# Moving the start of the float32r operands in SBUF from 32 bytes past a multiple of 64 to a multiple of 64

## The chip, the cores and the metric

One NeuronCore of one Trainium2 chip runs the whole program in a single launch. The metric is the device time of one execution in microseconds (us). Its engines are TensorE (PE in the profile; its weight loads stand apart as PEld), VectorE (DVE), ScalarE (ACT), GpSimd (POOL) and SyncE (SP), which issues most DMAs. SBUF is the on-chip memory with 128 partitions; "an address" below is a byte address within a partition, and it is the same in all 128.

## The reference

Two transformer-like blocks run over 1024 tokens of 1024 features, all in float32. The first is a mixer of three branches (gated linear attention, an mLSTM memory, an S5 state space), merged by gates, and then a SwiGLU feed-forward net. The second has a latent-attention layer and a recurrent layer, each with an attention over 256 memory vectors.

```python
def first_block(x, c, ...):
    h = rms_norm(x, pre1_w[l]) * (1.0 + sc1) + sh1
    y = hybrid_mixer(h, w_in[l], ...)                  # products with 1024 x 6.7k weights, three branches
    x = x + (1.0 + gt1) * rms_norm(y, post1_w[l])
    h = rms_norm(x, pre2_w[l]) * (1.0 + sc2) + sh2
    gate, up = jnp.split(h @ ffn_w_in, 2, axis=-1)
    x = x + (1.0 + gt2) * rms_norm((silu(gate) * up) @ ffn_w_out, post2_w[l])

def second_block(x, mem, ...):                         # two layers
    z = h @ w_in;  tok = causal_attention(...) or rg_lru_branch(...)
    y = concat([tok, memory_attention(...)]) * silu(gate)
    h = layer_norm(ALPHA * h + y @ w_out, ln_g, ln_b)
```

## The kernel before

Nearly all the arithmetic is matrix products in a split form. Each float32 operand is kept as two tiles of type float32r, a high part (the rounded value) and a low part (what the rounding left): the activations are `ah` and `al`, a slot of weights is `wh` and `wl`, and other pairs are `gh`/`gl`, the two `yb`, and the parts in `tx`. One product is three TensorE matmuls, high by high, high by low and low by high, which `mm3` (by way of `mm`, whose matmul is L120) writes one after the other. So a stationary tile of 128 columns is loaded for every matmul. `ident` marks transposes (`tr`, L127), which are float32 matmuls of another form.

The moving operand of a float32r matmul is 512 columns wide (2048 bytes of a partition) in most products: `gemm_ws` for everything that is stored with features on partitions, and the FFN's output product `ffn_out`. It is 256 columns wide in three places: the output projections `w_out_pass` and the values `in_v`, where the moving operand is a weight slot; and the sums of quarters `tx` in `ffn_in`, where the 256 columns are two runs of 128 that lie apart. A few matmuls are plain float32: the profile's shapes write both types as f32, and names tell them apart. `xc,wg` and `acc,ones` are float32, as is everything of the S5, GLA and mLSTM cores.

Weights come from DRAM through `load_w`: the slot `wr` by DMA, ScalarE rounds it to `wh`, VectorE subtracts to give `wl`. `self.e()` gives a work tile of 128 x 1028 float32, of which 1024 columns are used, from a ring of four slots.

SBUF is filled from both ends. On the left lie the constants (pool `const`), then `act` with `ah` and `al`, then the pools that a stage opens. On the right lie the pools of a section: `wraw`, `whl`, then `ev`, which holds the work tiles. Every tile takes a multiple of 32 bytes. The address of a tile is therefore the sum of the tiles below it; the constants before `act` add up to a number that is 32 past a multiple of 64, and so do the pools at the right end. The tiles behind them are multiples of 64 bytes, but for the ring of work tiles: 1028 x 4 = 4112 bytes are rounded to 4128, which is 64 x 64 + 32. All slices that TensorE reads begin at multiples of 512 bytes from their tile's start. So all float32r operands, moving and stationary, begin 32 bytes past a multiple of 64, and the four slots of the ring begin at 0 and 32 past it in turn.

The order of the work on TensorE is written by the generators of the kernel and by the order in which they are stepped. Neither they nor the DMA queue look at an address.

Of the kernel before, what the change touches and what calls it, by code (L numbers as in the profile page):

```python
# [36 lines left out]
class Once:  # L37
    """Makes each of its items when it is first asked for."""
# [13 lines left out]
class Kernel:  # L52
# [8 lines left out]
    # Work is written as generators. The main one yields after each piece of work for TensorE; a  # L61
    # side one yields how many microseconds of other TensorE work its next piece should wait for.
# [87 lines left out]
    def silu2(self, out, x):  # L150
        """2 silu(x), from the tanh that shares its table with exp."""
        self.act(out, x, AF.Tanh, scale=0.5)
        self.stt(out, out, 1.0, x, ALU.add, ALU.mult)
# [9 lines left out]
    def section(self, es, raw, hl, e, width=1024):  # L163
        """Weight slots and float32 work tiles of a section, at the right end of SBUF."""
        self.ww = width
        self.wraw = self.pool("wraw", bufs=raw, es=es, side="right")
        self.whl = self.pool("whl", bufs=hl, es=es, side="right")
        self.ev = self.pool("ev", bufs=e, es=es, side="right")

    def e(self, dt=F32):  # L170
        return self.ev.tile([128, 1028], dt, tag="e", name="e")

    def load_w(self, src, n=1024):
        """One slot of weights: raw float32 from DRAM, split into two float32r parts."""
# [8 lines left out]
    def plan_w(self, *groups):  # L183
        """The weight slots the main generator will ask for, in order, in groups used together."""
# [13 lines left out]
    def gemm_ws(self, ps, w, x, nk, woff=0, halves=(0, 1)):  # L198
        """ps[128 features, 1024 tokens] from a stationary weight slot."""
# [17 lines left out]
    def gemm_pair(self, x, nk, first, rest):  # L217
        """Two column tiles, first halves first; waits for the tasks that form x's token halves."""
# [14 lines left out]
    def psc(self, ring=None):  # L233
        """One bank of PSUM, of four in turn; or of a ring of three (0), or the fourth (1)."""
# [5 lines left out]
    def rstd(self, pool, ss, n, eps, w=1):  # L240
        """(ss / n + eps) ** -0.5 on a narrow tile."""
# [7 lines left out]
    def to_act(self, src, t):  # L249
        """Token tile [128 tokens, 1024] -> act[:, :, tokens], split."""  # L250
# [15 lines left out]
    def setup(self):  # L266
        nc, A = self.nc, self.A
        self.const = self.pool("const")
        self.drp = self.pool("dr", space=DRAM)
        self.actp = self.pool("act")  # L270
# [36 lines left out]
        self.d_gq = dr("d_gq", [4, 128, 1024])   # q, q, k, k  # L307
        self.d_gc = dr("d_gc", [2, 128, 1024])   # cumulative log decay * 16
# [12 lines left out]
    def ada_vec(self, i, p, accp, wp):  # L321
        """Steps that form row vector i >= 2 of the adaLN table, broadcast over the partitions.

        A shift is mod, a scale or gate (1 + mod) * the norm's weight."""
# [29 lines left out]
    def start(self, es):  # L354
        """The first two column tiles of the input products, with h = rms(x) scale + shift into act.

        adaLN's first scale and shift come in by pieces of 256 features, and the products follow
        feature by feature."""
# [36 lines left out]
        def ada(ws):  # L395
            """Shift and scale of a block of features, before the sum over partitions."""
# [71 lines left out]
    def mem_load(self, es):  # L468
        """The memory, transposed and split."""
        p = self.pool("mkv", es=es)  # L470
        return self.mem_split([p.tile([128, 1024], F32R, name="mem%d" % i) for i in range(4)])

    def mem_split(self, t):
        """The memory's features by blocks of 128, high and low parts; t: two tiles of each part."""
# [6 lines left out]
    def mem_kv(self, l, x, tail=None):  # L481
        """Keys and values of the memory for layer l of the second block."""
# [47 lines left out]
    def in_v(self, b, qs=(0, 1)):  # L530
        """Values of branch b in token layout."""
# [18 lines left out]
    def log_sigmoid(self, a, x):  # L550
        """x <- min(x, 0) - log(1 + exp(-|x|)); a: scratch."""
# [5 lines left out]
    def local_sums(self, out, x, p):  # L557
        """Running sums over the tokens of each chunk of 128."""
# [5 lines left out]
    def in_misc(self, p1):  # L564
        """Gate inputs of both branches; GLA's log decays and their sums within chunks."""
# [38 lines left out]
    def conv(self, o, ps, w, b):  # L604
        """Causal convolution over four tokens, from PSUM."""
# [13 lines left out]
    def in_gate(self, b, func):  # L619
        """Gate of branch b, on its finished output."""  # L620
# [15 lines left out]
    def s5_pre(self, p, pt):  # L636
        """Small per-state values, [128 = (re, im) x 64 states, 32 groups]."""
# [25 lines left out]
        self.s5t = t("t", [128, 32])       # angle in turns  # L663
# [41 lines left out]
        # decay over a block of 8 steps, its angle, and powers 0..8 and 7..0  # L705
# [19 lines left out]
    def cossin(self, co, si, x, tmp):  # L725
        """cos and sin of 2 pi x; x is overwritten by its fraction in [-1/2, 1/2]."""
# [7 lines left out]
    def s5_core(self, hb, pm, pu, pt, su, turn):  # L734
        """Groups 4 hb .. 4 hb + 3."""
# [50 lines left out]
        # blocks of 8 steps  # L786
# [36 lines left out]
    def load_sy(self, b):  # L823
        """S5 output tile b as [channel, (step in block, block)]."""
# [6 lines left out]
    def s5_glu(self, p):  # L831
        """y * sigmoid(y @ w + b)."""
# [27 lines left out]
    def branch(self, b, p, ready=None, merged=None, first=False):  # L860
        """merged += 2 sigmoid(gate) * (y @ proj); ready: the task that forms y."""
# [38 lines left out]
    def gla_pair(self, pr, p1, p2, mD, ready):  # L900
        """Two heads of gated linear attention, chunks of 128 tokens, four chunks at a time.

        Within a chunk the decay between two tokens is split at the middle of the smallest aligned
        block that holds both, so that both exponents are <= 0: one product per block size."""
# [7 lines left out]
        for u in range(2):  # L912
# [55 lines left out]
            for li, m in enumerate(sizes):  # L968
# [3 lines left out]
                else:  # L972
                    # keys to the chunk's end, queries from its start
# [63 lines left out]
    def ml_rows(self, p):  # L1037
        """Per-token gate rows, [4 heads, 1024]."""
# [24 lines left out]
    def ml_core(self, p1, p2):  # L1063
# [6 lines left out]
        # per-token columns  # L1070
# [18 lines left out]
        for pr in range(2):  # L1089
            nc.gpsimd.memset(Sz, 0.0)  # L1090
            for u in range(2):
# [8 lines left out]
                # decays: exp(b_i - m_i + i_j - b_j), zero above the diagonal  # L1100
# [76 lines left out]
    def w_out_pass(self, store, evac, final, pre=None, tail=None):  # L1177
        """y[tokens, 1024] = act^T @ w by column quarters; the tasks of final are returned.

        The last two quarters go side by side over the tokens: the tiles are finished evenly."""  # L1180
# [37 lines left out]
    def block1_end(self, es, low, G, tx, tail, done):  # L1218
        """x1 = x + (1 + gt1) rms(y) w; h2 into act and tx. low, G: float32 tiles."""
# [42 lines left out]
    def to_tx(self, src, t, rb, tx):  # L1262
        """Token tile 4 + t -> the second halves of act and the sums of quarters with token tile t."""
# [25 lines left out]
    # The hidden features come by the Strassen-Winograd scheme: seven products of quarters in place  # L1289
    # of eight. Quarters of the weights: gate and up column tile by half of the contraction; of the  # L1290
    # activations: half of the contraction by half of the tokens.
    def ff_raw(self, i, fs):
        """Weights of a pair and their sums: g = A11, A12; u = A21 -> S3, A22; s = S1, S2."""
# [30 lines left out]
    def ffn_in(self, tx, fs, a, fin):  # L1324
        """a: the first pair, its first weights loaded."""
# [28 lines left out]
        def add(out, ps, x, a, b, h=0, g=0):  # L1354
            """out <- ps + x at columns a:b of halves h, g."""
# [86 lines left out]
    def ffn_out(self, es, slot):  # L1442
# [35 lines left out]
        def out(parts):  # L1478
            """Products of one group of hidden features, or of the last two."""
# [997 lines left out]
```

## Time and profile before

| | us |
|---|---|
| median of 3 runs | 2843.36 |
| lowest, highest | 2841.15, 2856.39 |
| span of the profiled execution | 2851.6 |
| TensorE busy in it | 2711.0 (95%) |
| weight loads | 2230.4 (78%) |
| VectorE busy | 1716.1 (60%) |
| ScalarE busy | 930.2 (33%) |
| GpSimd busy | 856.5 (30%) |

The profiled execution is its own run: its span, 2851.6 us, is 8.2 us over the median. The profile gives a start and a duration for every instruction. Matmuls are pipelined, so a matmul's duration is longer than the time from its start to the start of the next. What a stream of matmuls costs is that spacing, and it is read from starts in the timeline, or from the count of matmuls in a stretch without idle time.

### The profile page before, as it was taken

The page shows a single profiled execution, that of the slowest core. Times are in us where ns is not written, and L with a number is a line of the kernel's source. Part 1 is how long each engine was busy: PE and PEld are TensorE (multiplying, and loading weights), DVE is VectorE, ACT ScalarE, POOL GpSimd, SP SyncE. Part 2 cuts the span into 40 slices and gives each one's busy share as a digit, 9 for nine tenths or more (in the row PEclk, how much of TensorE's full clock was granted, in tenths as well). Part 3 has the DMA queues.
Part 4 walks back from the last instruction along what each step waited for, and adds up shares of the span by engine and source line. Part 5 has one row for each costly group of instructions (what it writes and reads, how often), then busy time and mean ns, then how long its engine had stood idle before and what let it go on. Part 6 is the DMA issues. An engine that isn't in the chain of part 4 may idle for free. (4 is left out here: it accounts for less than half of the span.)

```text
span 2851.6 us, 40682 instructions
## 1 busy us (share of the span) xinstructions
PE 2711.0 (95%) x16156; PEld 2230.4 (78%) x16156; DVE 1716.1 (60%) x2462; ACT 930.2 (33%) x1427; POOL 856.5 (30%) x767
## 2 busy tenths in 40 slices
PE   6989899999999999799999999999989998999998
PEld 5778688778878889698988888787766665976688
DVE  7886974553453244944544456653577776667586
ACT  6453544311111133422222321232333334146330
POOL 4694661000000002844444200131213547112332
PEclk8999999899999999899999999999999999999999
DMA  8323224444564242222222422242220113322231
GB/s 243 108 73 113 92 81 134 134 134 168 185 214 164 94 146 91 89 89 88 68 89 86 151 89 89 96 164 76 92 85 29 34 42 107 139 82 64 70 107 64
DMA packets 133901, 304.10 MB, mean 107 GB/s; under 512 B 18024, under 2 KB 61880, under 8 KB 133584
## 3 DMA queue, kind: packets, MB, share of 16 engines
q1 hardware_dynamic: 133712, 301.51, 31.5%
q8 instruction: 127, 2.08, 0.3%
q14 instruction: 62, 0.51, 0.1%
HBM read 226.17 MB, written 73.94 MB: 105 GB/s over the span
## 5 line engine op out<-in xcount | busy, mean ns | idle before, releaser
L120 PE MATMUL psg<-ah,wh 128*128 128x512 f32 x1392 | 563.5, 406 | 21.6 <-ACT wh L1311 9.3
L120 PE MATMUL psg<-ah,wl 128*128 128x512 f32 x1392 | 558.0, 401 | 3.5 <-DVE wl L136 3.5
L120 PE MATMUL psg<-al,wh 128*128 128x512 f32 x1392 | 557.8, 401 | 2.1 <-DVE al L136 2.0
L136 DVE TENSOR_TENSOR wl<-wr,wh 128x1024 fp32r<-128x1024 f32 (+3 forms) x212 | 272.1, 1285 | 379.3 <-ACT wh L179 262.8
L179 ACT CAST wh<-wr 128x1024 fp32r<-128x1024 f32 (+3 forms) x161 | 162.3, 1010 | 798.7 <-PE psg L120 379.5
L120 PEld LDWEIGHTS psg<-ah,wh 128*128 128x128 f32 x1392 | 265.8, 191 | 92.7 <-issue 12.3
L120 PEld LDWEIGHTS psg<-al,wh 128*128 128x128 f32 x1392 | 266.6, 191 | 66.1 <-issue 5.5
L120 PEld LDWEIGHTS psg<-ah,wl 128*128 128x128 f32 x1392 | 266.5, 191 | 64.5 <-DVE wl L136 3.7
L120 PE MATMUL psc<-wh,ah 128*128 128x256 f32 x1024 | 290.5, 284 | 7.8 <-DVE ystore L136 4.3
L120 PE MATMUL psc<-wl,ah 128*128 128x256 f32 x1024 | 287.2, 281 | 0.0
L120 PE MATMUL psc<-wh,al 128*128 128x256 f32 x1024 | 286.7, 281 | 0.0
L142 POOL TENSOR_SCALAR rsv<-ss 128x1 f32<-128x1 f32 x32 | 12.8, 400 | 757.2 <-DVE ss L1238 514.0
L120 PEld LDWEIGHTS psc<-wh,ah 128*128 128x128 f32 x1024 | 196.7, 192 | 13.0 <-DVE ystore L136 5.0
L120 PEld LDWEIGHTS psc<-wl,ah 128*128 128x128 f32 x1024 | 195.8, 191 | 0.3
L120 PE MATMUL psc<-tx,wh 128*128 128x256 f32 x1088 | 195.5, 280 | 0.0
L120 PEld LDWEIGHTS psc<-wh,al 128*128 128x128 f32 x1024 | 195.4, 191 | 0.1
L136 POOL TENSOR_TENSOR e<-e 128x1024 f32<-128x1024 f32 (+3 forms) x65 | 110.0, 1696 | 238.5 <-issue 112.0
L120 PEld LDWEIGHTS psc<-tx,wh 128*128 128x128 f32 x1088 | 170.0, 189 | 3.3
L136 POOL TENSOR_TENSOR acc<-acc,e 128x512 f32<-128x512 f32 (+2 forms) x60 | 116.2, 1936 | 158.3 <-PE psc L120 155.9
L120 PE MATMUL psc<-tx,wl 128*128 128x256 f32 x544 | 152.8, 281 | 0.0
L136 DVE TENSOR_TENSOR e<-psc,e 128x512 f32<-128x512 f32 (+1 forms) x138 | 89.9, 666 | 103.4 <-PE psc L120 103.2
L120 PE MATMUL psc<-wh,gh 128*128 128x512 f32 x352 | 139.5, 398 | 2.5 <-ACT gh L1459 2.5
(479 smaller groups left out, 5484.5 us busy)
## 6 DMA issues: line engine op xcount, KB each, us to landing
wr<-in_w_ws_dram SPq DMA_DIRECT2D x45, 512.0 KB
wr<-in_ffn_in_dram SPq DMA_DIRECT2D x44, 512.0 KB
aw<-in_ada_w_dram SPq DMA_DIRECT2D x32, 512.0 KB
wr<-in_w_out_dram SPq DMA_DIRECT2D x24, 512.0 KB
d_h<-e SPq DMA_DIRECT2D x22, 512.0 KB
wr<-in_ffn_out_dram SPq DMA_DIRECT2D x22, 512.0 KB
e<-d_h SPq DMA_DIRECT2D x22, 512.0 KB
e<-d_y SPq DMA_DIRECT2D x20, 512.0 KB
```

Source lines behind the costliest of these rows:

```text
L120: self.nc.tensor.matmul(out, lhsT, rhs, start=start, stop=stop)
L136: (eng or self.nc.vector).tensor_tensor(out=out, in0=a, in1=b, op=op)
L142: (eng or self.nc.vector).tensor_scalar(out=out, in0=a, scalar1=s1, scalar2=s2, op0=op0, op1=op1)
L179: (self.nc.vector.tensor_copy if self.hi_dve else self.nc.scalar.copy)(hi[:, :n], raw[:, :n])
```

## The change

Two tiles of 8 float32 (32 bytes) that nothing writes or reads are allocated, `padl` between the constants and `act` on the left, and `padr` as the first tile on the right. The work tile shrinks from 1028 to 1024 columns. All else in the diff removes comments and docstrings (left out here). There is no new instruction, and no operand changes its shape or type.

```diff
     def e(self, dt=F32):
-        return self.ev.tile([128, 1028], dt, tag="e", name="e")
+        return self.ev.tile([128, 1024], dt, tag="e", name="e")
...
     def setup(self):
         nc, A = self.nc, self.A
         self.const = self.pool("const")
         self.drp = self.pool("dr", space=DRAM)
+
+        self.pool("padl").tile([128, 8], F32, name="padl")
+        self.pool("padr", side="right").tile([128, 8], F32, name="padr")
         self.actp = self.pool("act")
```

After it every float32r operand begins at a multiple of 64 bytes: those on the left lie 32 bytes higher, those on the right 32 lower. The work tiles take 4096 bytes each, so that the four slots of the ring begin alike.

## Rows read from the trace of the kernel before

**Rows 1.** The page's busy times, and TensorE's clock in 40 slices of the span.
```profile
PE 2711.0 (95%) x16156; PEld 2230.4 (78%) x16156; DVE 1716.1 (60%) x2462; ACT 930.2 (33%) x1427; POOL 856.5 (30%) x767
...
PEclk8999999899999999899999999999999999999999
```

**Rows 2.** Busy us (count) of PE, PEld, DVE, ACT, POOL; clock, DMA, GB/s, by stage.
```profile
600.00:1000.00 400.00, 399.80 (x1754) 323.14 (x1753) 161.18 (x174) 67.52 (x74) 0.00 (x0) 1.00 0.45 157
1200.00:2000.00 800.00, 794.48 (x4287) 680.91 (x4285) 420.05 (x514) 222.70 (x279) 233.08 (x147) 1.00 0.29 98
0.00:400.00 400.00, 338.56 (x3148) 288.05 (x3149) 324.17 (x564) 203.10 (x392) 243.48 (x354) 0.92 0.39 122
2000.00:2400.00 400.00, 382.96 (x1839) 258.47 (x1839) 281.01 (x494) 153.77 (x244) 165.70 (x96) 1.00 0.19 60
```

**Rows 3.** Groups by line and shape: xcount, busy us, mean ns, idle before.
```profile
L120 PE MATMUL psg<-ah,wh 128*128 128x512 f32 x1392 | 563.5, 406 | 21.6 <-ACT wh L1311 9.3 <-ACT ah L424 8.4 <-DVE e L145 3.1
...
L120 PE MATMUL psc<-wh,ah 128*128 128x256 f32 x1024 | 290.5, 284 | 7.8 <-DVE ystore L136 4.3 <-ACT e L544 2.6 <-ACT P L951 0.5
...
L120 PE MATMUL psc<-tx,wh 128*128 128x256 f32 x1088 | 195.5, 280 | 0.0
...
L120 PE MATMUL psc<-tx,wl 128*128 128x256 f32 x544 | 152.8, 281 | 0.0
L120 PE MATMUL psc<-wh,gh 128*128 128x512 f32 x352 | 139.5, 398 | 2.5 <-ACT gh L1459 2.5
...
L120 PE MATMUL psg<-yb,wh 128*128 128x512 f32 x384 | 121.0, 395 | 0.0
...
L120 PE MATMUL psc<-al,wh 128*128 128x512 f32 x256 | 101.4, 396 | 2.2 <-DVE al L136 2.2
...
L120 PE MATMUL psg<-yb,wl 128*128 128x512 f32 x192 | 75.7, 394 | 0.0
```

**Rows 4.** The view of rows 2, in four stretches of one shape each.
```profile
860.00:1020.00 160.00, 160.00 (x701) 131.29 (x700) 51.62 (x46) 25.12 (x25) 0.00 (x0) 1.00 0.35 119
1640.00:1840.00 200.00, 200.00 (x859) 161.15 (x858) 128.01 (x168) 40.27 (x46) 0.25 (x2) 1.00 0.26 90
1060.00:1110.00 50.00, 50.00 (x427) 50.00 (x426) 15.58 (x26) 12.53 (x40) 0.00 (x0) 1.00 0.36 122
2760.00:2840.00 80.00, 80.00 (x708) 80.00 (x708) 52.11 (x91) 8.12 (x8) 10.99 (x12) 1.00 0.17 63
```

**Rows 5.** Timeline of TensorE in the FFN's input product: start us, us, line, tiles.
```profile
1499.99 0.28 PE L120 MATMUL psc<-tx,wl 128*128 128x256 f32 x1
...
1501.41 0.28 PE L120 MATMUL psc<-tx,wl 128*128 128x256 f32 x1
```

**Rows 6.** Timeline of TensorE at half clock, 512 columns, about 124 us.
```profile
123.12 0.63 PE L120 MATMUL psg<-ah,wh 128*128 128x512 f32 x1
...
124.83 0.63 PE L120 MATMUL psg<-al,wh 128*128 128x512 f32 x1
```

**Rows 7.** Timeline of TensorE at half clock, 256 columns, about 407 us.
```profile
405.63 0.41 PE L120 MATMUL psc<-wh,ah 128*128 128x256 f32 x1
...
408.19 0.41 PE L120 MATMUL psc<-wh,ah 128*128 128x256 f32 x1
```

**Rows 8.** Timeline (merged) and group of float32 matmuls at full clock.
```profile
2545.60 2.74 PE L120 MATMUL psc<-xc,wg 128*128 128x512 f32 x6
...
L120 PE MATMUL psc<-xc,wg 128*128 128x512 f32 x5 | 2.3, 592 | 0.0
```

**Rows 9.** Timeline (merged) of eight transposes, and their durations min/median/max.
```profile
1120.34 1.03 PE L127 MATMUL psc<-ident,tx 128*128 128x128 f32 x8
...
L127 PE MATMUL psc<-ident,tx x96: 271/272/333, 1120.3 to 1890.9; 128*128 128x128 f32 x96
```

**Rows 10.** VectorE groups of one shape, without and with work tiles.
```profile
L136 DVE TENSOR_TENSOR tx<-tx,psc 128x512 f32<-128x512 f32 x144 | 97.2, 687 | 67.8 <-PE psc L120 67.8
...
L136 DVE TENSOR_TENSOR e<-psc,e 128x512 f32<-128x512 f32 x126 | 85.2, 690 | 100.9 <-PE psc L120 100.8
```

## The prediction, made before the result was known

> **What bounds the kernel now.** I read the page's busy times first, then the table by stages, then the groups by shape, and last the starts of single matmuls. TensorE is busy 95% of the span, and no other engine over 60% [rows 1]. By stages it is busy 99.9% of 600 to 1000 us and 99.3% of 1200 to 2000 us, at full clock, while the next busiest engine has about half of the time [rows 2]. So time that a matmul saves there is time that the kernel saves. Elsewhere TensorE waits a little: 338.56 of 400 us at the start, 382.96 of 400 in the attention [rows 2].
>
> A busy TensorE need not run at its peak, so the reader should look at the spacing of matmuls. In a stretch without idle time it is the length over the count, less the two counted matmuls that began before the stretch. At full clock, 2.4 GHz, 512 columns at one a cycle would take 213.3 ns and 256 columns 106.7 ns. Measured [rows 4]: 160 us / 699 = 228.9 ns (`ah`, `al` and `yb`, 512 columns), 200 / 857 = 233.4 (FFN output, 512), 50 / 425 = 117.6 and 80 / 706 = 113.3 (output projections, 256). The two-run `tx` takes (1501.41 - 1499.99) / 12 = 118.3 ns [rows 5]. So each float32r matmul costs 6.6 to 20 ns more than its columns. In units of 16 columns, which are 64 bytes and 6.67 ns, the first four spacings are 34.3, 35.0, 17.6 and 17.0, where the columns are 32 and 16. Operands repeat with a period of three matmuls, and the values lie near whole numbers of thirds.
>
> Two rows say what kind of excess this is. At half clock it is gone: (124.83 - 123.12) / 4 = 427 ns for 512 columns, (408.19 - 405.63) / 12 = 213.3 for 256, which are the columns at 1.2 GHz [rows 6, 7]. And float32 matmuls at full clock, which take two cycles a column, have almost none: six took 2.74 us and the last of them 592 ns, so they start (2740 - 592) / 5 = 430 ns apart against 426.7 [rows 8]. Whatever delays float32r hides where a column has twice the time. That is how an operand behaves that is fetched just too slowly, and an operand that begins 32 bytes past a multiple of 64 touches one 64-byte piece more than it has: 17 for 256 columns, 33 for 512.
>
> **The change part by part.** It adds no instruction and no wait. The two pads cost nothing in time, and no queue is moved past another. Three things can change.
>
> (a) The spacing of float32r matmuls. The bounds of an aligned one: no better than the columns with the small cost that float32 shows, 430 - 426.7 = 3 ns [rows 8], so 216.3 ns for 512 columns and 109.7 for 256; no gain on the other side, as now. Below nothing isn't excluded, see the rivals. The transposes bear on the 256 bound: eight, each with a load of 128 weight columns, took 1.03 us, the last of them 272 ns, so (1030 - 272) / 7 = 108.3 ns apart [rows 9]; weight loads can come that fast. I take the full gain for 512 columns, since the excess is nearer to one more piece for each operand or more than to a fixed cost. For 256 columns I take half, because the weight loads fill 80.00 of 80 us there [rows 4] and may hold the spacing themselves.
> - 512 columns: 3 x 1392 + 384 + 192 + 3 x 256 = 5,520 matmuls [rows 3] x (228.9 - 216.3) = 69.6 us.
> - FFN output: 3 x 352 = 1,056 [rows 3] x (233.4 - 216.3) = 18.1 us.
> - 256 columns: 3 x 1024 = 3,072 [rows 3] at the mean of 113.3 and 117.6, x 5.8 ns, and 1,088 + 544 = 1,632 of `tx` [rows 3] x 8.6 ns: 17.8 + 14.0 = 31.8, of which half is 15.9 us.
>
> Together 103.6 us. What of it lies on the path: in the two full stretches [rows 2] lie all of the FFN output, nearly all of `tx` (half of 14.0) and some 3,100 of the 5,520 (1,754 + 4,287 less 1,056, 1,632 and, an estimate, 250 others): 18.1 + 7.0 + 39.1 = 64 us, which is all saved, as the nearest engine would rise from 53% to about 56%. Of the other 39 us I take three quarters, since there TensorE waits for others in part and runs at half clock in part, where there is nothing to gain [rows 1, 2, 6]: 30 us. The sum is 94 us, 3.3%.
>
> On the page of the Trainium skill "TensorE: Matmul & The Clock Gate", section "Back-to-back issue gap", a stream at full clock is spaced by the columns over 2.4 and 2.5 ns, 215.8 ns for 512. The trace's 228.9 ns [rows 4] is 13 ns over that rule, its float32 cost of 3 ns [rows 8] agrees with the constant; by the rule the sum would be some 3 us larger.
>
> (b) The weight loads read their 128 columns from the same new starts. They are hidden behind matmuls of 512 columns (131.29 of 160 us [rows 4]), and in (a) for 256.
>
> (c) The ring of work tiles. Its slots begin at 0 and 32 past a multiple of 64 in turn now, and alike afterwards. VectorE takes 690 ns on them and 687 on `tx`, which is not in the ring [rows 10]: the start costs VectorE nothing that shows, and I count zero. If it did cost, VectorE's busy 60% leaves the cover.
>
> **The rivals.**
>
> *One piece less, no more.* Alignment takes away just the extra piece, 6.67 ns of each 512-column matmul, and the rest of the excess is the chip's own. Then 6,576 x 6.67 = 43.9 us, and with the 15.9 for 256 columns 60, of which nine tenths (as above) are saved: 54 us, 2789. For it: 34.3 and 35.0 are two and three pieces over 32 [rows 4], and misalignment explains only one. Against: nothing else is known that grows in such pieces.
>
> *Nothing.* The excess is the chip's rate for 4-byte operands at one column a cycle, wherever they begin, or the pads don't move what they should. Then the time stays at 2843. For it: 17.0 / 16 and 34.3 / 32 are nearly one ratio, which is how a rate looks, while a piece for each matmul would weigh twice as much in the shorter ones; and the same code with the same shapes runs at 117.6 in one stretch and 113.3 in another [rows 4], so the start of the operand isn't all. Against: the values in whole pieces, and the float32 rows can't tell, since they are too slow to show it [rows 8]. The page "SBUF — State Buffer" of the Trainium skill, section "Specifications (TRN2)", gives lines of 16 bytes; by that, starts at 32 and at 64 are both whole lines and the change would do nothing. No row here shows the length of a line.
>
> *Slower.* Now moving operands on the left and weights on the right begin in different halves of 128 bytes, if the tiles before are added up (32 and 96 past); afterwards both begin 64 past. If two reads that walk in step meet in the same half, each matmul falls into the slower of the modes that the trace shows: 233.4 in place of 228.9 and 117.6 in place of 113.3 [rows 4]. The price is 5,520 x 4.5 = 25 us and, on half of the 3,072, 1,536 x 4.3 = 7 us: 32 us, 2875. It decides from the point where the FFN's and the branches' stretches go over 229 ns. For it: the modes exist, at one start of operands. Against: in the output projections both modes have operands in different halves, so the halves don't pick the mode there.
>
> **How the numbers follow.** The profiled span is 2851.6 us, 8.2 over the median; the sum of 94 us is against it, and 2851.6 - 94 = 2757.6 there; against the median it is 2843.4 - 93.7 = 2749.7. Forecast: chance 0.45, with its own range from 2710 (all of the 256 columns' 31.8 us too, and all of it on the path: 87.7 + 31.8 = 119.5, and 600 matmuls of the attention like the rest, 8 us, some 130 in all) to 2775. One piece: 0.22, 2775 to 2805. Nothing: 0.22, 2838 to 2850. Slower: 0.11, 2858 to 2880. Faster by over 0.5% (14 us, about what a measurement of this kernel can tell from no change) is 0.67, within it 0.22, slower 0.11. Left out are the ends above 2850 and below 2708: about 0.11 and 0.04.
>
> **What would show it.** In the profile after, the stretches of rows 4: 160 us should hold some 740 of the 512-column matmuls (216 ns); at 720 (222 ns) the rival of one piece holds, at 699 nothing has changed, below 690 the slower mode has come. For 256 columns 80 us should hold 720 to 740. The half-clock spacing and the float32 spacing should stay at 427 and 430 ns; VectorE's 690 too. If the spacings fall as said but the span by much less than 94 us, the share on the path is what I had wrong, and waits of TensorE for `wh`, `wl` or the work tiles would have grown. The forecast falls if the spacing of 512 columns stays over 226 ns.

## The result, and the profile after

The changed kernel takes 2871.87 us (2871.12 to 2874.89) where the kernel before, measured beside it, takes 2847.30 (2841.15 to 2856.39): a ratio of 1.0092, 95% interval 1.0072 to 1.0113. It is 24.6 us slower, where 94 us less were forecast.

The profiled execution of the changed kernel spans 2869.6 us, 18.0 more than that of the kernel before, which lay over its median. So what is read from this pair of profiles below explains 18 us of the 24.6. First the page's busy times, which answer [rows 1]:

```profile
PE 2732.3 (95%) x16156; PEld 2238.2 (78%) x16156; DVE 1723.2 (60%) x2462; ACT 931.0 (32%) x1427; POOL 851.4 (30%) x767
```

TensorE has the same 16,156 matmuls and is busy 21.3 us longer; the other engines stand within 8 us of where they were. Then the two full stages, which answer [rows 2] (busy us and count of PE, PEld, DVE, ACT, POOL, then clock, DMA share, GB/s), and the four stretches of one shape, which answer [rows 4], with a fifth inside the last projection:

```profile
600.00:1000.00 400.00, 399.80 (x1725) 319.83 (x1724) 160.92 (x177) 65.44 (x72) 0.00 (x0) 1.00 0.45 156
1200.00:2000.00 800.00, 791.35 (x4250) 677.01 (x4250) 426.00 (x515) 221.86 (x280) 228.31 (x149) 0.99 0.28 95
...
860.00:1020.00 160.00, 160.00 (x690) 129.77 (x689) 52.84 (x47) 26.55 (x26) 0.00 (x0) 1.00 0.35 119
1640.00:1840.00 200.00, 199.56 (x858) 161.50 (x859) 124.77 (x164) 44.13 (x53) 0.08 (x1) 1.00 0.29 100
1060.00:1110.00 50.00, 50.00 (x419) 50.00 (x418) 17.26 (x26) 13.85 (x39) 0.00 (x0) 1.00 0.45 149
2760.00:2840.00 80.00, 79.51 (x639) 78.13 (x638) 51.09 (x79) 14.17 (x16) 9.72 (x8) 1.00 0.27 99
2780.00:2815.00 35.00, 35.00 (x294) 35.00 (x294) 16.16 (x31) 4.21 (x4) 0.00 (x0) 1.00 0.10 32
```

TensorE is nearly as full as before and simply gets through fewer matmuls. By the prediction's own reading, 160 us / 688 = 232.6 ns for 512 columns (228.9 before), 50 / 417 = 119.9 and 79.51 / 637 = 124.8 for the output projections (117.6 and 113.3). The last figure is too high, because the last window now catches matmuls of the stage ahead of the projection; inside the projection, from 2780 to 2815 us, it is 35 / 292 = 119.9. Only the FFN's output gained a little: 199.56 / 856 = 233.1 against 233.4.

What the prediction wanted to see unchanged is unchanged. The timeline (start us, us, line, tiles) gives the half clock of [rows 7] as (410.05 - 407.49) / 12 = 213.3 ns once more, the six float32 matmuls of [rows 8] take 2.74 us again, and VectorE's two groups of [rows 10] stay at 684 and 689 ns. The `tx` products of [rows 5], which were to gain, come every (1511.87 - 1508.67) / 27 = 118.5 ns, where 118.3 stood (117.8 over longer stretches of them):

```profile
1508.67 0.28 PE L120 MATMUL psc<-tx,wl 128*128 128x256 f32 x1
...
1511.87 0.28 PE L120 MATMUL psc<-tx,wl 128*128 128x256 f32 x1
...
407.49 0.41 PE L120 MATMUL psc<-wh,ah 128*128 128x256 f32 x1
...
410.05 0.41 PE L120 MATMUL psc<-wh,ah 128*128 128x256 f32 x1
...
2563.83 2.74 PE L120 MATMUL psc<-xc,wg 128*128 128x512 f32 x6
...
L136 DVE TENSOR_TENSOR tx<-tx,psc 128x512 f32<-128x512 f32 x144 | 96.9, 684 | 67.0 <-PE psc L120 66.4
L136 DVE TENSOR_TENSOR e<-psc,e 128x512 f32<-128x512 f32 x126 | 85.0, 689 | 100.3 <-PE psc L120 100.3
```

Where the time came from is seen best by following single matmuls. The program's order is the same in both kernels, so the n-th matmul of one trace can be set against the n-th of the other (starts in us, read from the timelines):

```
matmul   before   after   behind   what runs up to there
 4,500    603.3    604.4    +1.1   inputs and cores; TensorE waits, or has half its clock
 6,000    946.2    952.9    +6.7   branches, 512 columns
 6,500   1051.1   1059.7    +8.6   branches, then memory
10,000   1605.3   1619.3   +14.1   output projection, FFN input
11,000   1834.5   1846.2   +11.8   FFN output
13,500   2375.6   2390.1   +14.5   latent attention
14,500   2519.3   2537.2   +17.9   second output projection
15,500   2766.0   2779.9   +14.0   recurrent layer
16,155   2840.2   2858.5   +18.3   last output projection
```

The loss grows where TensorE is full. From 4,500 to 6,000 it is 1,500 x 3.7 ns = 5.6 us, and 5.6 are read; in the last projection it is 655 x 6.6 ns = 4.3 us, and 4.3 are read. Where TensorE waits for others, as in the first 600 us and in the recurrent layer, little is lost or something comes back. The FFN's output, where TensorE is full, gives 2.3 us back; its shorter spacing explains 1 us of that at most, and the rest wasn't traced.

### The profile page after: what moved, and what is told of

Same layout as the page of the kernel before. It is cut to its first block, busy times and chain, and to the rows that moved or that the text cites. A ratio compares the mean times of both kernels' runs of the same rounds, so it can differ in the third digit from the quotient of the medians.

```text
span 2869.6 us, 40682 instructions
## 1 busy us (share of the span) xinstructions
PE 2732.3 (95%) x16156; PEld 2238.2 (78%) x16156; DVE 1723.2 (60%) x2462; ACT 931.0 (32%) x1427; POOL 851.4 (30%) x767
## 5 line engine op out<-in xcount | busy, mean ns | idle before, releaser
L136 DVE TENSOR_TENSOR wl<-wr,wh 128x1024 fp32r<-128x1024 f32 (+3 forms) x212 | 280.8, 1326 | 378.4 <-ACT wh L179 259.9
```

What stands on the lines that cost most here:

```text
L136: (eng or self.nc.vector).tensor_tensor(out=out, in0=a, in1=b, op=op)
```

## The experiments

Three theories stood at first. Theory 1: the moving operand and the weights disturb each other when they begin in the same half of 128 bytes. Theory 2: each operand's own start within 64 bytes counts. Theory 3: the narrower work tiles cost the time. The addresses are added up from the tiles, by which `ah` begins 32 past a multiple of 256 before and the weight slots 224; no run prints an address, and what bears the sums out is that the kernels show the spacings of streams whose distance is set within one tile (below). "Distance" below is the start of the moving operand less that of the stationary one, modulo 256 bytes. In the output projections and the FFN's output the weights are the moving operand, so there the sign turns: 64 in the branches is 192 there.

### Starts shifted on one side or the other

Four kernels move the starts with unused tiles alone (columns of 4 bytes; the work tiles are 1024 wide as in the changed kernel).

```diff
 # the changed kernel
 self.pool("padl").tile([128, 8], F32, name="padl")
 self.pool("padr", side="right").tile([128, 8], F32, name="padr")
 # e1: padl 16 columns, no padr     e2: padl 8, padr 24 columns
 # e3: padl 8, no padr              e4: no padl, padr 8
```

> The pads are 64 bytes on the left and none on the right: all float32r operands again begin 32 bytes past a multiple of 64, as in the kernel before, but moving operands and weights now begin in the same half of 128 bytes (96 and 96 past), as in the changed kernel (64 and 64). If two reads that begin in the same half get in each other's way (theory 1), the spacing of 512-column matmuls is the changed kernel's, 232.4 ns, and the time 2865 to 2880 us. If the start within 64 bytes makes the spacing (theory 2), it is the old 228.9 ns and 2835 to 2855 us. If it is the ring of work tiles (theory 3), which is 1024 wide here, also 2865 to 2880, with the spacing at 228.9.

> The pads are 32 bytes on the left and 96 on the right: all float32r operands begin at multiples of 64 bytes, as in the changed kernel, but moving operands and weights in different halves of 128 bytes (64 and 0 past). Theory 1 (same half) expects the old spacing of 228.9 ns and 2835 to 2855 us; theory 2 (the start within 64 bytes) expects 232.4 ns and 2865 to 2880 us.

> Only the operands on the left are moved by 32 bytes to multiples of 64; those on the right stay 32 past (64 and 96 past a multiple of 128). If the start within 64 bytes counts for each operand by itself (theory 2), the products with the left operand moving go to about 232.4 ns and the output projections and the FFN's output product, whose moving operand is on the right, keep 113.3 and 233.4 ns: about 2860 us. If only the distance of the two counts (theory 1), it is a distance of 32 that no run has shown: between 2840 and 2880, and the same in both kinds of product.

> Only the operands on the right are moved by 32 bytes to multiples of 64; those on the left stay 32 past (32 and 64 past a multiple of 128). By theory 2 the output projections (moving operand on the right) go to 119 or 120 ns and the products with the left operand moving keep 228.9: about 2855 us. By theory 1 the same distance of 32 as with the left ones alone, the other way round, and so the same spacings as there.

Measured: e1 1.0075 (1.0060 to 1.0090), e2 1.0040 (1.0026 to 1.0054), e3 1.0107 (1.0091 to 1.0123), e4 1.0099 (1.0081 to 1.0118). The branch stretch and first projection of e1, then of e2:

```profile
860.00:1020.00 160.00, 160.00 (x690) 129.90 (x690) 52.85 (x47) 26.15 (x26) 0.00 (x0) 1.00 0.35 119
1060.00:1110.00 50.00, 50.00 (x423) 50.00 (x423) 17.40 (x27) 14.28 (x41) 0.00 (x0) 1.00 0.45 157
```
```profile
860.00:1020.00 160.00, 160.00 (x688) 129.25 (x687) 52.65 (x47) 26.20 (x26) 0.00 (x0) 1.00 0.35 119
1060.00:1110.00 50.00, 50.00 (x443) 50.00 (x443) 17.60 (x27) 14.22 (x41) 0.00 (x0) 1.00 0.49 169
```

e1 leaves every start 32 past a multiple of 64, as before the change, and still has the 690 matmuls of the changed kernel. So theory 2 falls: where each operand begins within 64 bytes isn't what costs. The two kernels aren't alike in everything: e1's first projection takes 50 / 421 = 118.8 ns, the changed kernel's 119.9. e2 is what theory 1 can't explain. Its operands lie in different halves again, and yet its 512-column branches take 160 / 686 = 233.2 ns and its first projection 50 / 441 = 113.4, while before it was 228.9 and 117.6. What does fit is the distance: in e2 the 64 of the branches and the 192 of the projections have changed places. e3 and e4 have one operand moved and the other not, in opposite ways, and agree with each other in the branches, the FFN's output and the projections.

### The ring of work tiles alone

```diff
-        return self.ev.tile([128, 1028], dt, tag="e", name="e")
+        return self.ev.tile([128, 1024], dt, tag="e", name="e")
```

> Theory 3 put to the test by itself: the float32 work tiles go from 1028 to 1024 elements of width, as in the changed kernel, and nothing else is changed, so every float32r operand begins where it did before (moving operands 32 bytes past a multiple of 128, weights 96 past). If the ring of work tiles is what costs (theory 3), this kernel takes 2865 to 2885 us, as the changed one. If the distance of the two operands costs (theory 1), it takes what the kernel before takes, 2841 to 2856 us, and the 512-column matmuls stay at some 229 ns in ah and yb and at 233 ns in the FFN's output.

Measured: 2846.20 us, ratio 1.0000 (0.9986 to 1.0015). Theory 3 falls. One thing was not expected. The `tx` products, whose addresses nobody touched, come every (1511.84 - 1509.46) / 21 = 113.3 ns in this profile, where they took 118.3 [rows 5]. Its second projection went the other way: 2440 to 2480 us hold 343 matmuls, where the kernel before has 356.

```profile
1509.46 0.28 PE L120 MATMUL psc<-tx,wl 128*128 128x256 f32 x1
...
1511.84 0.28 PE L120 MATMUL psc<-tx,wl 128*128 128x256 f32 x1
```

### The price by itself

Two kernels hold nothing but streams of 48 matmuls. `d` is the distance, in the first with the weights at a multiple of 128 bytes (`s00`) or 32 past one (`s32`; there 96 and 112 stand for 224 and 240).

```python
for r in range(2):
    for k in range(8):
        for a, b in ((0, 0), (0, 1), (1, 0)):    # high by high, high by low, low by high
            nc.tensor.matmul(ps[:, 0:n], weights(a, k), moving(b, k), ...)
```

> The disputed price by itself. The kernel leaves the whole of the reference's computation out (its output is copies of the input) and holds nothing but streams of 48 float32r matmuls, in the order high by high, high by low, low by high over eight blocks, each stream with a distance of its own between the start of the moving operand and that of the weights (0 to 112 bytes, modulo 128), the weights at a multiple of 128 bytes or 32 past one, 512 or 256 columns, and two repeats; then streams with weights of 32 or 64 columns in place of 128, and bfloat16 streams. Theory 1 (the two operands' distance): distance 0 gives 232.4 ns and 118.6 ns for 512 and 256 columns, distance 64 gives 228.9 or 233.3 and 113.3 or 117.8, distance 32 gives 233.3 to 234.3 and 118 to 120, at both starts of the weights; the streams with the same distance agree whatever the start. Theory 2 (the start of each operand by itself): streams agree by the start, not by the distance. If the excess over the columns' time (213.3 and 106.7 ns) comes from the weights being read beside the moving operand, it shrinks with the weights' columns: at 32 columns to about a quarter, 4 to 5 ns for 512; if it belongs to the moving operand alone it stays at 16 to 20 ns. In bfloat16, where rows are half as long, the same two ends hold.

> The streams of e6 once more, with the weights at multiples of 512 bytes and the moving operand 0 to 240 bytes past one in steps of 16 (and at 24, 56, 72, 120, 136, 320 and 448). It leaves out the whole of the reference's computation. Theory 4, formed from e1 to e6: a matmul's spacing goes by the signed distance, moving operand less weights, modulo 256 bytes. Then 64 gives 228.9 ns for 512 columns and 117.8 ns for 256 (both as in e6), 192 gives 233.3 and 113.3, 128 gives 232.4 and 118.7 to 120, 160 gives 234.2 and 118.0, 240 gives 226.7 and 117.0, 224 gives 233.4 and 118.3, and 320 and 448 repeat 64 and 192. If instead the modulus is 128 (theory 1 as it was put), 192 repeats 64, 128 repeats 0 (226.7 and 120.0), 160 repeats 32 (233.3 and 116.7) and 240 repeats 112 (231.1 and 113.3). If streams settle into one of several modes by chance, the two repeats of a distance differ. Streams whose weights don't move on from block to block: were the excess over the columns' time (213.3 and 106.7 ns) owed to where the next weights lie, it would change there; owed to the moving operand alone, it stays. Streams whose weights lie by turns 0 and 128 bytes past a multiple of 512, with the moving operand 64 past: if each matmul's spacing goes by its distance from the weights that are loaded beside it, the two values of 64 and 192 alternate.

In the timeline of such a kernel one row is one stream, so the next row's start less its own, over 48, is the price of a matmul (x47 means that one record is missing). From the first of the two kernels:

```profile
261.92 11.57 PE L49 MATMUL n512d004s00x<-big 128*128 128x512 f32 x48
273.32 11.37 PE L49 MATMUL n512d008s00x<-big 128*128 128x512 f32 x48
...
700.60 11.27 PE L49 MATMUL n512d000c32x<-big 128*32 128x512 f32 x48
711.71 11.34 PE L49 MATMUL n512d032c32x<-big 128*32 128x512 f32 x48
...
767.11 5.82 PE L49 MATMUL n256d000c32x<-big 128*32 128x256 f32 x48
772.76 5.79 PE L49 MATMUL n256d032c32x<-big 128*32 128x256 f32 x48
...
811.13 10.52 PE L49 MATMUL bf512d032x<-half 128*128 128x512 bf16 x47
821.49 10.52 PE L49 MATMUL bf512d064x<-half 128*128 128x512 bf16 x47
831.85 5.40 PE L49 MATMUL bf256d000x<-half 128*128 128x256 bf16 x48
837.09 5.40 PE L49 MATMUL bf256d032x<-half 128*128 128x256 bf16 x48
842.33 5.40 PE L49 MATMUL bf256d064x<-half 128*128 128x256 bf16 x48
```

Streams at one distance agree between the two starts of the weights, 229.4 ns at 64 for both. Distance 0 took 226.7 and not the 232.4 that theory 1 had told. Distance 4 costs 11.40 / 48 = 237.5 ns, the most of all for 512 columns. Weights of 32 columns at distance 0 still cost 11.11 / 48 = 231.5, and 5.65 / 48 = 117.7 for 256 columns, so the excess over 213.3 and 106.7 doesn't shrink to a quarter with what a load reads, as it would if the load's length were its cause. The bfloat16 streams take 10.36 / 48 = 215.8 (216.0 at distance 0) and 5.24 / 48 = 109.2 ns: they don't feel it. From the second kernel (weights at multiples of 512):

```profile
75.82 11.36 PE L44 MATMUL n512d064x<-big 128*128 128x512 f32 x48
87.02 11.26 PE L44 MATMUL n512d080x<-big 128*128 128x512 f32 x48
...
418.80 11.04 PE L44 MATMUL n512d000x<-big 128*128 128x512 f32 x48
429.68 11.28 PE L44 MATMUL n512d016x<-big 128*128 128x512 f32 x48
...
463.19 11.16 PE L44 MATMUL n512d064x<-big 128*128 128x512 f32 x48
474.19 11.25 PE L44 MATMUL n512d080x<-big 128*128 128x512 f32 x48
...
507.58 11.32 PE L44 MATMUL n512d128x<-big 128*128 128x512 f32 x48
518.74 11.36 PE L44 MATMUL n512d144x<-big 128*128 128x512 f32 x48
...
552.38 11.35 PE L44 MATMUL n512d192x<-big 128*128 128x512 f32 x48
563.57 11.42 PE L44 MATMUL n512d208x<-big 128*128 128x512 f32 x48
...
720.59 5.85 PE L44 MATMUL n256d128x<-big 128*128 128x256 f32 x48
726.27 5.85 PE L44 MATMUL n256d144x<-big 128*128 128x256 f32 x48
...
743.32 5.62 PE L44 MATMUL n256d192x<-big 128*128 128x256 f32 x48
748.77 5.88 PE L44 MATMUL n256d208x<-big 128*128 128x256 f32 x48
...
805.97 11.04 PE L44 MATMUL one512d000x<-big 128*128 128x512 f32 x48
816.85 11.17 PE L44 MATMUL one512d064x<-big 128*128 128x512 f32 x48
```

Worked out in the same way for all sixteen distances (ns, the second of two repeats):

```
distance     0    16    32    48    64    80    96   112   128   144   160   176   192   208   224   240
512 cols 226.7 231.5 233.5 233.1 229.2 231.0 233.5 231.0 232.5 233.1 234.4 233.3 233.1 234.4 233.3 226.9
256 cols 119.8 118.8 116.7 118.3 117.9 120.0 120.0 113.3 118.3 118.8 117.3 119.2 113.5 119.4 118.1 117.3
```

This is the kernels' table, in the main. 64 is the branches before, 228.9, and 128 the branches after, 232.6. 192 is the FFN's output before, 233.4, and the fast projections, 113.3. 96 and 160 are e3 and e4, whose branches took 160 / 685 = 233.6 and whose FFN output 100 / 427 = 234.2. For 256 columns not every entry fits: the first and last projection of the changed kernel, at 128, take 119.9, where the table has 118.3, and the last one of e3 and of e4, at 160, 35 / 295 = 118.6, where it has 117.3. A modulus of 256 fits, since 192 isn't 64 and 128 isn't 0, and 320 repeats 64 (11.00 / 48). Weights that stay at one place change nothing (10.88 / 48 = 226.7). With the weights 0 and 128 past by turns and the moving operand 64 past, 512 columns take 231.3 on average, between the prices of 64 and 192; 256 columns take 113.3, which is not between the table's 117.9 and 113.5.

One distance can have two prices, though. The first repeat of 64 took 11.20 / 48 = 233.3, the second 11.00 / 48 = 229.2, in the same program at the same places in SBUF; and 448, which should repeat 192, gave 117.8 in place of 113.5 for 256 columns. Between the two kernels of streams some other distances differ likewise: 48 took 230.0 ns for 512 columns in the first of them, and 16 took 113.3 for 256. Theory 4 is therefore: the spacing goes by the distance modulo 256, with two values at some distances, 64 and 192 among them, and for 256 columns 128 (118.8 in e1, 119.9 in the changed kernel) and 160 too. The table holds the one that its streams happened to show.

### The distance alone, and the starts alone

```diff
 # e9: the kernel before, and ahead of act
+        self.pool("padl").tile([128, 48], F32, name="padl")
 # e10: the changed kernel with padr of 56 columns, not 8     e11: with padl of 40 columns, not 8
```

> The kernel before with one unused tile of 192 bytes ahead of the activations: every moving operand and every weight then begins 224 bytes past a multiple of 256, at a distance of 0, in the same half of 128 bytes as in the changed kernel, where the distance was 128. Theory 4: the 5,520 products of 512 columns with moving activations go from 228.9 to 226.7 ns (12.1 us less), the 1,056 of the FFN's output from 233.3 to 226.7 (7.0 us less), the 3,072 of 256 columns with stationary activations from 113.3 to 120.0 (20.6 us more) and the 1,632 of tx from 117.8 to 120.0 (3.6 us more): 5 us more in sum, some 2852 us where the kernel before takes 2847. Theory 1 as it was put (same half of 128 bytes is bad, as in the changed kernel and e1): some 2871 us, and 232.4 ns in all 512-column stretches.

> The changed kernel with its right-hand unused tile 224 bytes long in place of 32: every float32r operand still begins at a multiple of 64 bytes (moving operands 64 past a multiple of 128, weights at one), but the signed distance modulo 256 is back at that of the kernel before, 64. Theory 4 (the distance): the spacings of the kernel before come back, 228.9 ns in the 512-column branch products, 233.3 in the FFN's output, 113.3 or 117.8 in the output projections, and the time is that of the kernel before, 2840 to 2856 us. If it is the starts at multiples of 64 that cost, whatever the distance, it takes what the changed kernel takes, 2865 to 2878 us.

> The changed kernel with its left-hand unused tile 160 bytes long in place of 32: every float32r operand still begins at a multiple of 64 bytes, all of them in the same half of 128 bytes as in the changed kernel, but at a distance of 0 modulo 256 in place of 128. Theory 4: the spacings of e9 come back, 226.7 ns in the 512-column branch products and in the FFN's output, 120.0 in the output projections, and about e9's time, 2840 to 2856 us. If sharing a half of 128 bytes costs, or the starts at multiples of 64, it takes 2865 to 2878 us.

Measured: e9 2846.53 us, ratio 0.9997 (0.9982 to 1.0012); e10 2843.43, 0.9992 (0.9979 to 1.0006); e11 2850.59, 1.0008 (0.9995 to 1.0020). First e10, then e11, in the branches, the FFN's output and the first projection:

```profile
860.00:1020.00 160.00, 160.00 (x701) 131.28 (x700) 50.51 (x46) 26.58 (x26) 0.00 (x0) 1.00 0.35 119
1700.00:1800.00 100.00, 100.00 (x430) 80.60 (x429) 68.57 (x91) 19.49 (x20) 0.00 (x0) 1.00 0.26 90
1060.00:1110.00 50.00, 50.00 (x427) 50.00 (x426) 17.12 (x28) 12.49 (x40) 0.75 (x2) 1.00 0.28 97
```
```profile
860.00:1020.00 160.00, 160.00 (x707) 132.48 (x707) 52.61 (x47) 26.57 (x26) 0.00 (x0) 1.00 0.35 119
1700.00:1800.00 100.00, 100.00 (x443) 82.81 (x442) 67.07 (x91) 17.54 (x19) 0.00 (x0) 1.00 0.25 85
1060.00:1110.00 50.00, 50.00 (x419) 50.00 (x418) 15.91 (x27) 12.04 (x38) 0.31 (x2) 1.00 0.29 102
```

These settle that the distance counts and the starts by themselves don't. e10 begins every operand at a multiple of 64, as the changed kernel does, and differs from it in the distance alone: it has the 701 and 427 matmuls of [rows 4] and the time before. e11 has them at multiples of 64 and in one half of 128 bytes, and loses nothing: at distance 0 the 512 columns take 160 / 705 = 227.0 and 100 / 441 = 226.8, which pays for the projections' 119.9. e9 has the same counts, 707, 443 and 419, with all starts 32 past. In time the table did less well: of e9 5 us more were told, and its interval ends at 1.0012, 3.4 us. So theory 1 as it was put, the same half, falls too; it was right about the changed kernel by the accident that its distance is 128.

### Two values at one distance, and a version with what has one

e8 shifts `tx` by 128 bytes and the hidden tiles by 64 more; e12 and e13 are the kernel before, unchanged; e14 takes e5 and shifts the hidden tiles `gh` and `gl` alone.

```diff
 # e8, before ptx and before p2 in ffn_out
+                self.pool("txp", es=es).tile([128, 32], F32, name="txp")
+        self.pool("ffp", es=es).tile([128, 16], F32, name="ffp")
 # e14, on e5, before p2 in ffn_out
+        self.pool("ffp", es=es).tile([128, 48], F32, name="ffp")
```

> The kernel before with two unused tiles on the left side of SBUF, 128 bytes ahead of the FFN's tiles (tx) and 64 bytes ahead of its hidden tiles (gh, gl). Theory 4 (the spacing goes by the signed distance, moving operand less weights, modulo 256 bytes): the 1,632 tx products go from a distance of 64 to 192, from 117.8 to 113.3 ns, 7.3 us in sum; the 1,056 products of the FFN's output from 192 to 0, from 233.3 to 226.7 ns, 7.0 us; everything else stays. Together 14 us less, some 2833 us where the kernel before takes 2847, a ratio of 0.995; the stage of the FFN's input gets shorter by 7 us and that of its output by 7 us. No operand begins at a multiple of 64 bytes in it, so by the change's own reason (starts at multiples of 64 help, theory 2) nothing moves: 2847 us.

> The kernel before once more, unchanged, for a second profiled execution. In the first one the tx products of the FFN's input (256 columns, distance 64) came every 117.8 ns; in e5, which has the same addresses of those operands, and in e10, which has the same distance, they came every 113.3 to 113.7. Theory 5: at the distances 64 and 192 a stream of matmuls settles in one of two modes (228.9 or 233.3 ns, 113.3 or 117.8 ns), and which one isn't set by the addresses but by how the stream happens to start; then this execution or the next shows 113.3 in the tx products, or 117.8 in output projections that had 113.3, and its span differs from the first by up to 4.5 ns x 1,632 = 7 us. If the addresses alone set the spacing, every group has the value of the first execution to 0.2 ns: 117.8 for tx, 113.3 in both later output projections, 233.3 in the FFN's output.

> The kernel before a third time, as e12: by theory 5 any of the groups at distances 64 and 192 may show either of its two values; by the addresses alone all are as in the first execution.

> The kernel before with work tiles of 1024 columns (as e5, which changed nothing in the time) and one unused tile of 192 bytes ahead of the FFN's hidden tiles: only the 1,056 products of the FFN's output move, from a distance of 192 to 0 modulo 256. Distance 0 has shown one value alone, 226.7 ns, where 192 has 233.3: 7 us less, a ratio of 0.9975. The groups at 64 and 192 that stay may fall into either mode. If the gain is given back to another wait, the ratio is 1.000 and the stretch of the FFN's output is shorter all the same.

Measured: e8 2844.96 us, ratio 0.9991 (0.9979 to 1.0003), 2.5 us in place of 14; e14 2841.10, 0.9982 (0.9968 to 0.9997). The FFN's output of e8 and of e14, then the last projection (2780 to 2815 us) of e12 and of e13:

```profile
1700.00:1800.00 100.00, 100.00 (x443) 82.81 (x442) 67.07 (x91) 15.60 (x16) 0.00 (x0) 1.00 0.27 91
```
```profile
1700.00:1800.00 100.00, 100.00 (x443) 82.81 (x442) 69.35 (x92) 19.52 (x20) 0.00 (x0) 1.00 0.27 90
```
```profile
2780.00:2815.00 35.00, 35.00 (x299) 35.00 (x299) 16.66 (x31) 2.10 (x2) 3.31 (x4) 1.00 0.04 17
```
```profile
2780.00:2815.00 35.00, 35.00 (x311) 35.00 (x310) 17.69 (x32) 2.11 (x2) 3.67 (x4) 1.00 0.04 17
```

The FFN's output went from 233.4 to 100 / 441 = 226.8 ns in both, as told. The `tx` products of e8 went to distance 192 and stayed at 117.8, the other of its values: that is the half of the forecast that failed. e12 and e13 show that in one group the value isn't the program's to choose: in the same kernel the last projection took 35 / 297 = 117.8 ns in one execution and 35 / 309 = 113.3 in the next. Theory 5 holds for that group. The `tx` products had 117.8 in all three profiles of the kernel before and 113.3 in e5, e10 and e14, at the same distance. Over all profiles with `tx` at 64 or 192, the slow value goes with work tiles of 1028 columns (the three, and e8) and the fast one with 1024 (those, and e2 with (1482.58 - 1480.20) / 21 = 113.3). So for this group the program may have a say, by the ring; one profile each of four kernels doesn't prove it, and how the ring could do it isn't shown. e14, which moves only the FFN's output, to a distance that showed one value throughout, gained 5.1 us where 7 were expected, and is a little faster than both kernels. The 5.1 can be put down to the FFN's output, but not beyond doubt: the interval ends just short of 1, e8 has the same gain there and 2.5 us in all, and the `tx` products of e14 showed 113.3 as well (e5 showed that too and gained nothing in its median, with a slower second projection).

## Why the prediction was wrong

- **The bound.** Right. TensorE was the limit, and what each matmul lost in the branches and the last projection the kernel lost, matmul for matmul in the table of starts.
- **The step that failed** is the one from "an operand behaves that is fetched just too slowly" to "an operand that begins 32 bytes past a multiple of 64 touches one 64-byte piece more than it has", on which (a) rests. It gave each operand a price of its own, and from that came the term of 5,520 matmuls that were to fall from 228.9 to 216.3 ns. They rose to 232.6. e1 and the changed kernel have different starts and one spacing, 232.6; e10 and the kernel before have different starts and one spacing, 228.9. What counts is the distance of the two operands, and none of the distances tried brings 512 columns below 226.7 ns. Of the excess of 15.6 ns (228.9 less 213.3), 13.4 are there at every distance tried; the forecast took 12.6 of the 15.6 away. The clue was in the prediction's own hand, under "Nothing": 17.0 / 16 and 34.3 / 32 look like a rate. Each at its best distance, both shapes stand at it, 226.7 = 213.3 x 17/16 and 113.3 = 106.7 x 17/16. The Trainium skill's page "TensorE: Matmul & The Clock Gate", section "Back-to-back issue gap", has the columns over 2.4, and 2.5 ns, as the gap of an isolated matmul, and about 131 ns at 512 columns for a stream of loads and matmuls; the prediction took the first for a stream. The bfloat16 streams here, with a load for each matmul, do take the first, 215.8 and 109.2 ns, and not 131, so there the measurement decides; no float32r stream came near either.
- **Half clock and float32.** The reading that the excess hides where a column has twice the time held: 213.3 ns again after the change. It was true of any slow fetch and couldn't tell a start from a distance.
- **(b) The weight loads.** That they would hold half of the gain for 256 columns wasn't borne out: at distance 0 loads of a quarter the size leave 256 columns at 117.7 ns, where full ones take 119.8, and bfloat16 matmuls with full loads come every 109.2 ns.
- **(c) The ring.** Right: zero by e5, and VectorE's 684 and 689 ns.
- **The rival that came.** "Slower" had the sign and nearly the size: 32 us were priced and 24.6 came. That the size is so near is in part luck: it foresaw 233.4 ns, where the branches took 232.6, and 117.6 in half of the projections, where two of three took 119.9. With the measured spacings the sum is 5,520 x (232.6 - 228.9) = 20.4, the FFN's output 1,056 x (233.1 - 233.4) = -0.3, the projections 3,072 x 4.9 = 15.1 (three stretches, a mean of 114.6 before and 119.5 after), together 35 us, of which 24.6, or 0.7, arrived. By the prediction's own shares, all of what lies in the full stages (3,100 x 3.7 less 0.3, some 11 us) and three quarters of the rest, 29 would have; so the share outside, an estimate, was nearer to a half. Some of the 15.1 hangs on which value the projections before held: with 117.8 in the last one, as in e12, it is less. Its rule was too simple (the half; e11 is in one half too and loses nothing). And the argument against it was not one: that the projections show two spacings at one pair of starts is the two values of one distance, which says nothing on whether the halves, or the distance, matter. With it the rival was given 0.11.
- **The page beside the rival "Nothing".** The Trainium skill's page "SBUF — State Buffer", section "Specifications (TRN2)", gives lines of 16 bytes, by which the change would do nothing. The starts by themselves did cost nothing, as e10 shows; what moved with them, the distance, cost 24.6 us. The same page of the Trainium skill, section "A bandwidth-pool intuition that's wrong (but worth ruling out)", lists a second, independent read port for weight loads beside the moving operand's. By that their distance shouldn't matter. The float32r streams don't agree, 226.7 to 237.5 ns by the distance alone; the bfloat16 ones do, 215.8 to 216.0 at the three distances tried.

What stays open is the mechanism. That the two starts count through their distance suggests that the reads of the two operands meet somewhere; no run says where, nor what picks between the two values of a distance.

## What to carry to other kernels

An operand's start is not a property to put right by itself: in a stream of float32r matmuls price the pair, moving less stationary start modulo 256 bytes, in a kernel of bare streams before a pad is added, and take a distance that shows one value (0 for 512 columns; 256 columns pay 119.8 there, and e9 and e11, with all operands at 0, gained nothing). A spacing that stands at one ratio to the columns for two sizes (17/16 here) looks like a rate, and no distance tried here got below it. Where one stage shows two spacings at the same addresses, leave the difference out of the sum: it can come or go with the next execution.

## What was not expected of the hardware

- At full clock, float32r matmuls of 512 columns are spaced 226.7 ns at best and 256 columns 113.3, 17/16 of their columns at 2.4 GHz; bfloat16 ones 215.8 to 216.0 and 109.2, at distances of 0, 32 and 64 alike.
- The distance of the two operands adds up to 10.8 ns to that for 512 columns (237.5 at 4 bytes) and, for 256, at the distances that are multiples of 16, up to 6.7 (120.0 at 80 and 96).
- At some distances a stream holds one of two values: for 256 columns 113.3 or 117.8 ns at 64 and at 192, for 512 columns at 64 229.2 or 233.3 (the slower in one bare stream alone). In the last projection it differed between executions of one program.
